# Dense products of a hybrid decoder layer: split and evacuation passes over 1024 columns, pair sums in neighbouring PSUM banks, and six gate-row chunks placed inside the input projection

## The chip, the cores and the metric

The kernel runs on one core of a Trainium2 chip. The metric is the device time of one execution in microseconds. Three executions of the kernel before gave 1505.12, 1505.9 and 1506.55 us, so the median is 1505.9 us; less is better.

## The reference

One decoder layer for 256 tokens of width 2048, all in float32. What matters here, cut from the reference:

```python
mod = c_act @ w_ada[l] + b_ada[l]
sh1, sc1, g1, sh2, sc2, g2 = jnp.split(mod, 6, axis=-1)
h = _modulate(_rmsnorm(x, norm1_g[l]), sh1, sc1)
proj = h @ w_in[l]                       # 256 x 2048 by 2048 x 4928
...
o_a = ...                                # gated linear recurrence, 8 heads, from four blocks of proj
qh = (_rmsnorm(q_a, q_a_norm_g[l]) @ w_q_up[l])
kv = (_rmsnorm(kv_a, kv_a_norm_g[l]) @ w_kv_up[l])
o_b = ...                                # causal attention, 8 heads
mix = jnp.concatenate([o_a, o_b], axis=-1) @ w_out[l]
x = x + g1[:, None, :] * mix
h2 = _modulate(_rmsnorm(x, norm2_g[l]), sh2, sc2)
y = _hier_moe(h2, ...)                   # top 2 of 8 experts in the best of 4 groups
x = x + g2[:, None, :] * y
```

`mod` is a vector of six pieces of 2048: shifts, scales and gates of the two halves of the layer. It is called "ada" below, after its weights.

## The kernel before, in words

**Weights.** All weights come through one ring of buffers of 128 x 4096 float32 (2 MB each). The list `items` gives the order; `ring_fill` (L172) issues the next load on SyncE's queue as soon as a buffer is free, and `ring_done` frees a buffer when the last instruction that reads it has ended. The ring has four buffers (`RING`), two more from the first pieces of the output projection on, and a seventh from the experts on. The experts read 192 chunks in a fixed order, 403 MB of the 571 MB that pass through this queue.

**Dense products.** `dense` (L410 to L435) multiplies 256 tokens by 320 to 512 columns, in the manner of float32 on fp32r matmuls: both factors are split in a high and a low part, and three products are summed. For each 128 rows of weights (`kt`) ScalarE writes the high part (L417), VectorE writes the low part (L418), and TensorE runs six matmuls of 512 columns (L432 to L434, three for each half of the tokens) or, turned, twelve of 256 columns (L425 to L427). The two sums stand in two PSUM tiles of one bank each (`pw`, four buffers), so two products can be in flight. The function `end` empties them: in the input projection ScalarE copies (L455) or VectorE adds to the sum so far (L457), one instruction for each bank.

**Input projection.** `w_in` handles ten blocks of columns in four quarters of the rows, the first quarter in two halves. Beside it, `adt_chunk` works out the shifts and scales of the first norm on VectorE: 24 instructions over 2048 columns (L271), two to a weight chunk, at lower priority than the rest.

**Other ada chunks.** `ada_chunk` (L283 to L296) multiplies the other four pieces (`g1`, `sh2`, `sc2`, `g2`, eight chunks of 2 MB each) on TensorE with one output row, into a bank of their own. A chunk is eight matmul instructions, which the trace records as 16. `EARLY` and `SPREAD` say after which items of the list how many of these 32 chunks stand. `ada_end` empties the bank; for `g1` these are four additions of one row on VectorE (L302).

**Order.** The instructions of each engine are put in order by the scheduler of the tile framework from the program order, priorities and buffers. Each engine then runs its list in order and waits where a semaphore is missing.

**Stages.** Input projection until about 235 us; attention (`mla`) and recurrence (`hgrn`), two of each, with the last quarter of the input projection, until about 450 us; output projection (`w_out`) until about 560 us; routing; then the experts.

Of the kernel before, what the change touches and what calls it, by code (L numbers as in the profile page):

```python
# [17 lines left out]
P = 128  # L18
D = 2048

RING, NARENA, NTEMP, NSPLIT, RING2 = 4, 14, (8, 6), 4, 2

SPREAD = (1, 4, 7, 5, 5, 2, 0, 0, 0, 2, 1, 1, 0)
EARLY = {33: 1}
# [21 lines left out]
def tile_hybrid_layer(ctx, tc, A, out):  # L46
# [6 lines left out]
    psum = ctx.enter_context(tc.tile_pool(name="psum", bufs=1, space=PSUM))  # L53
    late = ExitStack()
# [26 lines left out]
    def pw(name="pw"):  # L81
        return psum.tile([P, 512], F32, tag="w", bufs=4, name=nm(name))
# [327 lines left out]
    def dense(wt, ncol, kts, lhs, end, turned=False):  # L410


        ps = [pw("pacc") for _ in range(2)]
        for i, kt in enumerate(kts):
            w = wt[:, i * ncol:i * ncol + ncol]
            s = splits.tile([P, 2, 512], F32R, tag="s", name=nm("split"))
            S.activation(s[:, 0, :ncol], w, AF.Copy)  # L417
            V.tensor_sub(s[:, 1, :ncol], w, s[:, 0, :ncol])  # L418
# [16 lines left out]
        end(ps)  # L435

    def w_in(it):
# [5 lines left out]
        for n in ns:  # L443
# [6 lines left out]
            def end(ps):  # L450
                if fresh:
                    proj[n] = big([P, 2, 512], "proj")
                for t in range(2):
                    if fresh:
                        S.activation(proj[n][:, t, :ncol], ps[t][:, :ncol], AF.Copy)  # L455
                    else:
                        V.tensor_add(proj[n][:, t, :ncol], proj[n][:, t, :ncol], ps[t][:, :ncol])  # L457
# [109 lines left out]
    def w_out(half, j):  # L567
# [6 lines left out]
        def end(ps):  # L574
            if half == 0:
                mix0[j] = big([P, 2, 512], "mix0")
                for t in range(2):
                    S.activation(mix0[j][:, t], ps[t], AF.Copy)
                return
            m = mix0.pop(j)  # L580
            for t in range(2):
                V.tensor_add(m[:, t], m[:, t], ps[t])
                V.tensor_mul(m[:, t], m[:, t], gate[:, 512 * j:512 * j + 512])
                V.tensor_add(x2[j][:, t], x2[j][:, t], m[:, t])
# [122 lines left out]
    def mla(g):  # L707
# [11 lines left out]
        def keep(dst, n, o):  # L719

            def end(ps):
                for t in range(2):
                    S.activation(dst[:, t], ps[t][:, :n], AF.Copy)
                    if o is None:
                        continue
                    sq = tmp([P, 512], "sq")
                    S.activation(sq[:, :n], ps[t][:, :n], AF.Square)
# [139 lines left out]
    split_stack.close()  # L867
    ringC = late.enter_context(tc.tile_pool(name="ringC", bufs=1, side="right"))
# [338 lines left out]
```

## Time and profile before

| what | value |
|---|---|
| median of three runs | 1505.9 us |
| the profiled execution, its own time | 1505.27 us |
| its span, first to last instruction | 1503.0 us |
| mean granted TensorE clock | 0.888 of full speed |
| TensorE matmul busy | 1127.9 us, 75% |
| VectorE busy | 588.6 us, 39% |
| ScalarE busy | 338.4 us, 23% |
| bytes moved by DMA | 575.61 MB, 383 GB/s over the span |

The profile shows one execution. Busy time is the union of an engine's instructions. A matmul's row lasts longer than the distance to the next matmul's start, since matmuls overlap, so the pace of TensorE is read from starts. The chain is followed back from the last instruction to what released each step. [...]

### The profile page before, as it was taken

The numbers are of one execution on the slowest core, as the hardware profiler recorded it, in microseconds if no ns is written. First come the engines' busy times: TensorE is split into PE (matmuls) and PEld (weight loads), VectorE is DVE, ScalarE is ACT, GpSimd is POOL, SyncE is SP. The second block draws the span as 40 slices with busy tenths as digits, with TensorE's granted clock in tenths as the row PEclk, the third lists the DMA queues.
The fourth block names the chain that finished last, engine by engine and source line by source line (L and its number), as shares of the span: only waits on it lengthen the run. The fifth ranks groups of instructions, "written<-read, shape, count | busy, mean of one in ns | idle before, by whom it ended". The sixth has DMA issues, their size and how long they took to land.

```text
span 1503.0 us, 22846 instructions
## 1 busy us (share of the span) xinstructions
PE 1127.9 (75%) x9893; PEld 687.8 (46%) x9893; DVE 588.6 (39%) x1200; ACT 338.4 (23%) x699; POOL 5.0 (0%) x9
## 2 busy tenths in 40 slices
PE   5989999979999989675666666657657756666556
PEld 2868887737568756333323323323423423332222
DVE  4699998769765552220120121113112112112112
ACT  5634446536435423000100100100100100000000
POOL 0000000000000000000000000000000000000000
PEclk7999999989999999888888888879888889779787
DMA  9788796877979798999999999999999999999995
GB/s 373 263 332 356 298 352 257 315 302 313 369 293 376 293 373 343 430 429 430 430 430 430 430 430 429 429 431 430 430 430 430 430 431 430 430 429 429 431 430 222
DMA packets 44143, 575.61 MB, mean 383 GB/s; under 512 B 4858, under 2 KB 5114, under 8 KB 8712
## 3 DMA queue, kind: packets, MB, share of 16 engines
q1 hardware_dynamic: 42496, 570.56, 91.4%
q10 hardware_dynamic: 1544, 3.56, 0.6%
q8 instruction: 79, 1.29, 0.3%
q14 instruction: 24, 0.20, 0.0%
HBM read 572.00 MB, written 2.11 MB: 382 GB/s over the span
## 4 chain that ended last, share of the span: by engine, by line
DMA 51%; PE 37%; DVE 9%; ACT 1%; issue 1%; SPq 0%; ACTq 0%; DVEq 0%
DMA wch<-in_w_gu_dram 37%; DMA wch<-in_w_down_dram 13%; PE pgu L1040 5%; PE pacc L433 5%; PE pacc L434 5%; PE pacc L432 5%; PE pada L293 3%; PE py L1016 3%; PE pcmb L993 2%; PE pgat L970 2%; DVE wch L271 2%; DVE split L418 2%; DVE proj L457 1%; PE pacc L427 1%; PE pacc L425 1%; PE pacc L426 1%
## 5 line engine op out<-in xcount | busy, mean ns | idle before, releaser
L1040 PE MATMUL pgu<-wch,XT 128*32 128x256 f32 x4096 | 309.7, 455 | 201.0 <-DMA wch<-in_w_gu_dram 201.0
L1040 PEld LDWEIGHTS pgu<-wch,XT 128*32 128x32 f32 x4096 | 139.2, 126 | 361.0 <-DMA wch<-in_w_gu_dram 253.9
L1016 PE MATMUL py<-wch,hT 128*32 128x256 f32 x2048 | 167.9, 485 | 76.8 <-DMA wch<-in_w_down_dram 72.1
L1020 DVE TENSOR_TENSOR Y<-py,gate 32x256 f32<-32x256 f32 x256 | 107.6, 420 | 216.5 <-PE py L1016 213.6
L1005 DVE TENSOR_TENSOR hid<-sgu,pgu 128x128 f32<-128x128 f32 x32 | 9.2, 287 | 462.2 <-ACT sgu L1003 462.2
L418 DVE TENSOR_TENSOR split<-wch,split 128x512 fp32r<-128x512 f32 (+2 forms) x248 | 159.5, 666 | 69.6 <-ACT split L417 69.0
L417 ACT ACTIVATE split<-wch 128x512 fp32r<-128x512 f32 (+2 forms) x248 | 148.0, 614 | 161.2 <-PE pacc L434 98.4
L1016 PEld LDWEIGHTS py<-wch,hT 128*32 128x32 f32 x2048 | 78.9, 133 | 155.0 <-issue 60.8
L1003 ACT ACTIVATE sgu<-pgu 128x128 f32<-128x128 f32 x32 | 8.9, 277 | 602.5 <-PE pgu L1040 602.5
L975 ACT ACTIVATE XT<-pgat,sh,a 128x128 f32<-128x128 f32 x128 | 48.1, 456 | 223.1 <-PE pgat L970 223.0
L433 PE MATMUL pacc<-split,hhi 128*128 128x512 f32 (+1 forms) x192 | 75.5, 393 | 7.0 <-DVE split L418 7.0
L425 PE MATMUL pacc<-hhi,split 128*128 128x256 f32 x256 | 72.4, 286 | 2.8 <-ACT hhi L388 2.2
L426 PE MATMUL pacc<-hlo,split 128*128 128x256 f32 x256 | 72.7, 285 | 1.7 <-DVE hlo L389 1.7
L434 PE MATMUL pacc<-split,hlo 128*128 128x512 f32 (+1 forms) x192 | 73.7, 386 | 0.0
L432 PE MATMUL pacc<-split,hhi 128*128 128x512 f32 (+1 forms) x192 | 72.9, 392 | 0.8 <-DVE proj L457 0.7
L427 PE MATMUL pacc<-hhi,split 128*128 128x256 f32 x256 | 72.2, 285 | 1.1 <-DVE split L418 1.1
L293 PE MATMUL pada<-wch,ca 128*1 128x512 f32 x512 | 68.7, 602 | 3.3 <-DVE pada L288 3.3
L993 PE MATMUL pcmb<-Y,pwt 128*128 128x512 f32 x128 | 59.2, 605 | 15.5 <-DVE Y L1020 15.5
L970 PEld LDWEIGHTS pgat<-ohr,x 128*128 128x128 f32 x512 | 63.4, 205 | 10.7 <-issue 9.8
L970 PE MATMUL pgat<-ohr,x 128*128 128x128 f32 x512 | 66.8, 291 | 0.7 <-DVE sm L937 0.7
L271 DVE SCALAR_TENSOR_TENSOR wch<-wch,gate 128x2048 f32<-128x2048 f32 x24 | 54.8, 2284 | 0.0
L457 DVE TENSOR_TENSOR proj<-proj,pacc 128x512 f32<-128x512 f32 (+1 forms) x80 | 51.2, 662 | 0.8 <-PE pacc L434 0.4
(311 smaller groups left out, 1215.4 us busy)
## 6 DMA issues: line engine op xcount, KB each, us to landing
wch<-in_w_gu_dram SPq DMA_DIRECT2D x128, 2048.0 KB, 31.1
wch<-in_w_down_dram SPq DMA_DIRECT2D x64, 2048.0 KB, 31.5
wch<-in_w_ada_dram SPq DMA_DIRECT2D x36, 2048.0 KB, 10.1
wch<-in_w_ada_t_dram SPq DMA_DIRECT2D x12, 2048.0 KB, 7.9
wch<-in_w_in_dram SPq DMA_DIRECT2D x12, 2048.0 KB, 9.2
wch<-in_w_out_dram SPq DMA_DIRECT2D x8, 2048.0 KB, 9.5
wch<-in_w_in_h_dram SPq DMA_DIRECT2D x8, 1024.0 KB, 8.9
wch<-in_w_in_dram SPq DMA_DIRECT2D x3, 1664.0 KB, 7.0
```

The source lines that it names most:

```text
L293: PE.matmul(acc[b][32 * j:32 * j + 1, :], ca[:, kt:kt + 1], w[:, o:o + 512], start=kt == 0, stop=kt == 15)
L417: S.activation(s[:, 0, :ncol], w, AF.Copy)
L418: V.tensor_sub(s[:, 1, :ncol], w, s[:, 0, :ncol])
L426: PE.matmul(o, s[:, 0, c], lo, start=False, stop=False, skip_group_check=True)
L432: PE.matmul(o, hi[:, c], s[:, 0, :ncol], start=first, stop=False)
L433: PE.matmul(o, hi[:, c], s[:, 1, :ncol], start=False, stop=False)
L434: PE.matmul(o, lo[:, c], s[:, 0, :ncol], start=False, stop=stop)
L970: PE.matmul(ps[:, 128 * i:128 * i + 128], x2[kt // 4][:, t, 128 * (kt % 4):128 * (kt % 4) + 128], ohr[:, t], start=t == 0, stop=t == 1)
L993: PE.matmul(ps, PWT[G4][:, 128 * t:128 * t + 128], Y4[j // 2][:, 512 * (j % 2):512 * (j % 2) + 512], start=True, stop=True)
L1016: PE.matmul(py[32 * j:32 * j + 32, :256], H["T"][:, 32 * kt:32 * kt + 32], w[:, 1024 * kt + 256 * j:1024 * kt + 256 * j + 256], start=kt = ...
L1020: V.tensor_mul(Y[q][r:r + 32, 256 * j:256 * j + 256], py[32 * j:32 * j + 32, :256], gate[32 * j:32 * j + 32, c:c + 256])
L1040: PE.matmul(gu[32 * j:32 * j + 32, :256], XT[G4][kt // 8][:, kt % 8, 32 * e4:32 * e4 + 32], w[:, 1024 * i + 256 * j:1024 * i + 256 * j + 2 ...
```

## The change

Each split pass now covers 1024 columns where the weights allow it: two `kt` of 512 columns, four of 256, or two of 320 (640 columns). The split buffers are three of 1024 columns, where there were four of 512. The two sums of a product are one PSUM tile of two neighbouring banks, in a pool of two such tiles that is closed before the experts; an evacuation is one instruction over both banks. In the second half of the output projection three of four blocks are finished with instructions over 1024 columns, and the last one as before. The small temporary tiles are five, before six. The lists move five more of the `g1` chunks into the input projection: six stand there (after items 10, 17, 20, 24, 29 and 33 of the list), before one; after the items that follow there are 0, 3, 6, 5, 3, 2 in place of 1, 4, 7, 5, 5, 2.

```diff
-RING, NARENA, NTEMP, NSPLIT, RING2 = 4, 14, (8, 6), 4, 2
+RING, NARENA, NTEMP, NSPLIT, RING2 = 4, 14, (8, 5), 3, 2
-SPREAD = (1, 4, 7, 5, 5, 2, 0, 0, 0, 2, 1, 1, 0)
-EARLY = {33: 1}
+SPREAD = (0, 3, 6, 5, 3, 2, 0, 0, 0, 2, 1, 1, 0)
+EARLY = {10: 1, 17: 1, 20: 1, 24: 1, 29: 1, 33: 1}
...
-        ps = [pw("pacc") for _ in range(2)]
+        acc2 = psum_dense.tile([P, 2, 512], F32, tag="d", name=nm("pacc"))
+        ps = [acc2[:, 0], acc2[:, 1]]
+        some = 1024 // ncol // 2 * 2
         for i, kt in enumerate(kts):
-            w = wt[:, i * ncol:i * ncol + ncol]
-            s = splits.tile([P, 2, 512], F32R, tag="s", name=nm("split"))
-            S.activation(s[:, 0, :ncol], w, AF.Copy)
-            V.tensor_sub(s[:, 1, :ncol], w, s[:, 0, :ncol])
+            if i % some == 0:
+                n = ncol * min(some, len(kts) - i)
+                both = splits.tile([P, 2, 1024], F32R, tag="s", name=nm("split"))
+                w = wt[:, i * ncol:i * ncol + n]
+                S.activation(both[:, 0, :n], w, AF.Copy)
+                V.tensor_sub(both[:, 1, :n], w, both[:, 0, :n])
+            s = both[:, :, i % some * ncol:(i % some + 1) * ncol]
...
-        end(ps)
+        end(acc2)
...
-                for t in range(2):
-                    if fresh:
-                        S.activation(proj[n][:, t, :ncol], ps[t][:, :ncol], AF.Copy)
-                    else:
-                        V.tensor_add(proj[n][:, t, :ncol], proj[n][:, t, :ncol], ps[t][:, :ncol])
+                dst, src = proj[n][:, :, :ncol], ps[:, :, :ncol]
+                if fresh:
+                    S.activation(dst, src, AF.Copy)
+                else:
+                    V.tensor_add(dst, dst, src)
```

**VectorE, input projection, where the first `adt` passes run.** Before (`split` is the low part, L418; `proj` the sum so far, L457; `adt` a pass over 2048 columns, L271):

```order
L457 TENSOR_TENSOR proj_251<-proj_251,pacc_584 128x512
L418 TENSOR_TENSOR split_652<-wch_522,split_652 128x512
L457 TENSOR_TENSOR proj_251<-proj_251,pacc_585 128x512
L418 TENSOR_TENSOR split_661<-wch_522,split_661 128x512
L271 SCALAR_TENSOR_TENSOR wch_443,adt_642<-wch_443,gate 128x2048
L457 TENSOR_TENSOR proj_274<-proj_274,pacc_618 128x512
L457 TENSOR_TENSOR proj_274<-proj_274,pacc_619 128x512
```

and now (L424, L464 and L273 are the same three lines):

```order
L464 TENSOR_TENSOR proj_268<-proj_268,pacc_566 128x1024
L424 TENSOR_TENSOR split_606<-wch_523,split_606 128x1024
L424 TENSOR_TENSOR split_623<-wch_523,split_623 128x1024
L464 TENSOR_TENSOR proj_300<-proj_300,pacc_605 128x1024
L273 SCALAR_TENSOR_TENSOR wch_583,adt_653<-wch_583,gate 128x2048
```

Each pair of passes of 512 columns is one of 1024; the `adt` passes stand between them as they did.

**TensorE, the same place of the input projection.** The first of the six early chunks (`pada`) now stands between two products (before, no `pada` stood in this part of the list):

```order
L439 MATMUL pacc_566<-split_567,hhi_210 128x512
L440 MATMUL pacc_566<-split_567,hhi_210 128x512
L441 MATMUL pacc_566<-split_567,hlo_211 128x512
L295 MATMUL pada_593<-wch_485,ca 1x512 x8
L439 MATMUL pacc_605<-split_606,hhi_210 128x512
```

**VectorE, end of `g1`.** Before, its four additions (`brows`, L302) stood among the passes of the first recurrence (`b`, `d`: L501 to L504) and the end of the first attention (`o`, `mlo`):

```order
L201 TENSOR_SCALAR sm_2547<-sm_2547 128x8
L302 TENSOR_TENSOR brows_99<-brows_99,pada_1936 1x512
L202 TENSOR_TENSOR sm_2545<-sm_2545,sm_2547 128x8
L503 TENSOR_TENSOR d_478_2834<-b_2833 128x1024
L818 TENSOR_TENSOR o_2445<-o_2445,sm_2545 128x1024
L302 TENSOR_TENSOR brows_99<-brows_99,pada_1936 1x512 x3
```

and now they stand earlier, in the softmax of the first attention (`s`, `pT`):

```order
L806 TENSOR_REDUCE sm_2196<-s_2194 128x4
L464 TENSOR_TENSOR proj_268<-proj_268,pacc_2363 128x1024
L807 TENSOR_SCALAR sm_2196<-sm_2196 128x4
L304 TENSOR_TENSOR brows_102<-brows_102,pada_593 1x512 x4
L424 TENSOR_TENSOR split_2437<-wch_2395,split_2437 128x1024
L816 COPY pT_2208<-ppT_2203 128x512
```

They moved from behind the scan of the recurrence to ahead of the copy of the probabilities.

## Rows read from the trace of the kernel before

**Rows 1.** The page: span, and each engine's busy time.
```profile
span 1503.0 us, 22846 instructions
PE 1127.9 (75%) x9893; PEld 687.8 (46%) x9893; DVE 588.6 (39%) x1200; ACT 338.4 (23%) x699; POOL 5.0 (0%) x9
```

**Rows 2.** Stretches: length, busy time of PE, PEld, DVE, ACT, POOL, granted clock, DMA share, GB/s.
```profile
66.00:145.00 79.00, 70.15 (x414) 59.09 (x412) 77.26 (x125) 32.81 (x57) 0.00 (x0) 0.98 0.87 336
145.00:235.00 90.00, 87.22 (x526) 74.65 (x530) 83.37 (x141) 43.36 (x76) 0.00 (x0) 1.00 0.82 317
292.00:314.00 22.00, 14.30 (x109) 10.50 (x108) 20.00 (x35) 10.27 (x17) 0.95 (x1) 0.83 0.84 329
314.00:397.00 83.00, 81.83 (x538) 52.42 (x539) 55.59 (x112) 42.40 (x85) 0.96 (x1) 0.98 0.81 325
397.00:416.00 19.00, 13.13 (x109) 7.72 (x108) 18.91 (x33) 9.40 (x13) 0.42 (x1) 1.00 0.87 334
460.00:560.00 100.00, 98.65 (x509) 68.61 (x507) 54.61 (x99) 42.37 (x82) 0.00 (x0) 1.00 0.86 341
...
600.00:1503.00 903.00, 580.60 (x6413) 288.05 (x6413) 166.59 (x373) 56.00 (x165) 0.00 (x0) 0.84 0.99 421
```

**Rows 3.** The chain that ended last, from 160 to 225 us, shares by line.
```profile
by line: PE pacc L433 18.9%; PE pacc L434 18.5%; PE pacc L432 16.7%; PE pacc L426 11.6%; PE pacc L427 11.5%; PE pacc L425 11.2%; issue 3.6%; DVE proj L457 2.8%; DVE split L418 2.0%; ACT split L417 2.0%; DVE hlo L389 0.9%; DVE wch L271 0.2%;
```

**Rows 4.** The chain from 225 to 320 us, then from 320 to 460 us.
```profile
by line: PE pada L293 13.9%; PE pacc L434 11.8%; PE pacc L432 11.5%; PE pacc L433 11.2%; PE psc L788 2.8%; PE psc L786 2.8%; DVE brows L302 2.8%; DVE proj L457 2.6%; DVE b L501 2.5%; PE pov L810 2.2%; PE pqa L667 2.1%; PE pqk L765 2.0%; ACT
...
by line: PE pada L293 16.6%; PE pacc L432 11.9%; PE pacc L433 11.3%; PE pacc L434 10.8%; PE po L549 4.8%; PE po L551 4.2%; PE pA L527 3.5%; PE pov L810 2.2%; PE psc L786 1.9%; PE psc L788 1.9%; DVE split L418 1.9%; DVE b L501 1.7%; PE pqk L
```

**Rows 5.** Groups of VectorE from 66 to 145 us: count, busy, mean ns, idle before.
```profile
L271 DVE SCALAR_TENSOR_TENSOR wch<-wch,gate 128x2048 f32<-128x2048 f32 x14 | 32.0, 2284 | 0.0
L418 DVE TENSOR_TENSOR split<-wch,split 128x512 fp32r<-128x512 f32 x41 | 26.4, 684 | 0.3 <-ACT split L417 0.2
L457 DVE TENSOR_TENSOR proj<-proj,pacc 128x512 f32<-128x512 f32 x30 | 19.8, 682 | 0.2 <-PE pacc L434 0.2
```

**Rows 6.** Timeline of VectorE: start, length; runs of 512 columns, then passes of 1024.
```profile
66.89 1.89 DVE L418 TENSOR_TENSOR split<-wch,split 128x512 fp32r<-128x512 f32 x3
...
73.38 1.28 DVE L457 TENSOR_TENSOR proj<-proj,pacc 128x512 f32<-128x512 f32 x2
...
306.56 1.21 DVE L503 TENSOR_TENSOR d<-b 128x1024 f32<-128x1024 f32 x1
307.70 1.21 DVE L818 TENSOR_TENSOR o<-o,sm 128x1024 f32<-128x1024 f32 x1
308.94 2.09 DVE L302 TENSOR_TENSOR brows<-brows,pada 1x512 f32<-1x512 f32 x3
```

**Rows 7.** Timeline of TensorE in dense products: start, length.
```profile
481.98 0.40 PE L432 MATMUL pacc<-split,mhi 128*128 128x512 f32 x1
482.21 0.40 PE L433 MATMUL pacc<-split,mhi 128*128 128x512 f32 x1
```

**Rows 8.** The chain in order of time: one ada chunk on TensorE, start and length.
```profile
275.48 1.83 PE pada L293 x16
```

**Rows 9.** Groups from 60 to 225 us: matmuls that wait for the low part.
```profile
L433 PE MATMUL pacc<-split,hhi 128*128 128x512 f32 x104 | 42.7, 411 | 7.0 <-DVE split L418 7.0
```

**Rows 10.** ScalarE from 0 to 600 us: passes over 512 and over 1024 columns.
```profile
L417 ACT ACTIVATE split<-wch 128x512 fp32r<-128x512 f32 x224 | 137.7, 631 | 148.3 <-PE pacc L434 86.4 <-PE pacc L427 30.2 <-DMA wch<-in_w_in_dram 11.6
L506 ACT ACTIVATE d<-d 128x1024 f32<-128x1024 f32 x2 | 2.1, 1060 | 0.1
```

More of the change, by code (lines that the diff above doesn't have):

```diff
@@ L53, in tile_hybrid_layer @@
     psum = ctx.enter_context(tc.tile_pool(name="psum", bufs=1, space=PSUM))
+    dense_stack = ExitStack()
+    psum_dense = dense_stack.enter_context(tc.tile_pool(name="psum_dense", bufs=2, space=PSUM))
     late = ExitStack()
@@ L81, in pw @@
     def pw(name="pw"):
-        return psum.tile([P, 512], F32, tag="w", bufs=4, name=nm(name))
+        return psum_late.tile([P, 512], F32, tag="w", name=nm(name))
     def bc(ap, shape):
@@ L576, in end @@
                 mix0[j] = big([P, 2, 512], "mix0")
-                for t in range(2):
-                    S.activation(mix0[j][:, t], ps[t], AF.Copy)
+                S.activation(mix0[j], ps, AF.Copy)
                 return
             m = mix0.pop(j)
[L581 to L584, printed above, removed]
+            g = gate[:, 512 * j:512 * j + 512]
+            if j < 3:
+                V.tensor_add(m, m, ps)
+                V.tensor_mul(m, m, bc(g[:, None, :], [P, 2, 512]))
+                V.tensor_add(x2[j], x2[j], m)
+            else:
+                for t in range(2):
+                    V.tensor_add(m[:, t], m[:, t], ps[:, t])
+                    V.tensor_mul(m[:, t], m[:, t], g)
+                    V.tensor_add(x2[j][:, t], x2[j][:, t], m[:, t])
             x2_ready(j)
@@ L721, in end @@
             def end(ps):
+                S.activation(dst, ps[:, :, :n], AF.Copy)
+                if o is None:
+                    return
                 for t in range(2):
-                    S.activation(dst[:, t], ps[t][:, :n], AF.Copy)
-                    if o is None:
-                        continue
                     sq = tmp([P, 512], "sq")
-                    S.activation(sq[:, :n], ps[t][:, :n], AF.Square)
+                    S.activation(sq[:, :n], ps[:, t, :n], AF.Square)
                     V.tensor_reduce(ss[:, o + 4 * t:o + 4 * t + 4], sq[:, :n].rearrange("p (a b) -> p a b", a=4), AX.X, OP.add)
@@ L867, in tile_hybrid_layer @@
     split_stack.close()
+    dense_stack.close()
+    psum_late = late.enter_context(tc.tile_pool(name="psum_late", bufs=4, space=PSUM))
     ringC = late.enter_context(tc.tile_pool(name="ringC", bufs=1, side="right"))
```

## The prediction

> **What bounds the kernel now.** I read the page first [rows 1]: no engine is busy for more than 75% of the span, so the bound changes on the way. The stretches come next [rows 2]. From 600 us on the DMA engines are busy for 0.99 of the time at 421 GB/s: the experts stream weights and nothing else counts there. Their volume is fixed, so the whole kernel ends earlier by just as much as the part before 600 us ends earlier, and only that part can gain. Its bound alternates. From 66 to 145 us (stretch A) VectorE is busy 77.26 of 79 us and TensorE 70.15: VectorE is the bound. From 145 to 235 us (B) the chain is TensorE's own dense matmuls, 88% of it between 160 and 225 us [rows 3], though VectorE is at 83.37 of 90. From 225 to 460 us (C) the chain is mostly TensorE again, and its largest line is the ada matmuls, 13.9% and 16.6% [rows 4], with two islands (292 to 314 and 397 to 416 us) where VectorE is at 20.00 of 22 and 18.91 of 19 and TensorE idles. From 460 to 560 us (D) TensorE is at 98.65 of 100. DMA stays at 317 to 341 GB/s in these stretches, against 421 behind them.
>
> **Merged passes.** Their gain is smaller than mean durations suggest. Two passes of 684 ns against one of 1.21 us would be 0.16 us, but passes overlap: three splits run in 1.89 us, of which the last is 0.69, so one follows the other after 0.60; two additions out of PSUM take 1.28, the same step of 0.60 [rows 6]. A pass of 1024 is followed by the next after 307.70 − 306.56 = 1.14 us. A pair costs 1.20 before and 1.13 to 1.14 after: 0.07 us saved. A pass from PSUM over two banks has no row; at worst it saves nothing (two steps of 0.60), at best about this 0.07, which I take, since at 512 columns PSUM and SBUF cost the same.
> In A there are 41 splits and 30 additions of 512 columns [rows 5], some 35 pairs: 35 × 0.07 = **2.5 us off**, on the path because VectorE is the bound. The islands of C hold about six pairs: **0.4 us off**. In B, D and the rest of C TensorE leads and VectorE's saving is hidden behind it: 0. If that cover went, nothing would be added, since the passes only get shorter.
> [...]
> ScalarE's pass grows from 631 to about 1060 ns [rows 10] and halves in number. It is busy 32.81 of 79 us in A, so this costs nothing as long as a split is ready before TensorE asks. TensorE's six matmuls start 0.233 us apart [rows 7], so one `kt` lasts 1.40 us and a merged pair covers 2.80 us, against 1.06 on ScalarE and 1.14 on VectorE. With three buffers, two pairs (5.6 us) can be ready ahead, before three `kt` (4.2 us); an `adt` pass that stands between splits holds VectorE for 2.28 us. That can only shorten the 7.0 us of matmuls that waited for a low part [rows 9]; I book nothing for it and keep up to 7 us as the bound on the good side.
>
> **Moved ada chunks.** Five chunks leave C. One is 16 matmul records in 1.83 us [rows 8], so 9.15 us of TensorE. The chain holds ada matmuls for 13.9% of 95 us and 16.6% of 140 us, 13.2 + 23.2 = 36.4 us, of the 24 chunks × 1.83 = 43.9 us that stand there: 83% of an ada chunk is on the path. 9.15 × 0.83 = **7.6 us off**. Bounds: 9.15, and about 2 if the scheduler had put just these chunks into gaps.
> They come back in the input projection. By the dense matmuls that stand ahead of them in the changed list, three of the five fall into A and two into B. In A TensorE has 79 − 70.15 = 8.85 us free, and three chunks take 5.5: hidden, and 5.5 at most if that cover is gone. In B TensorE leads: 2 × 1.83 = **3.7 us added**, 0 at the least if they fill its gaps.
> Their loads move too: 5 × 2.1 MB, three of them (6.3 MB) into A. A moved 79 × 336 GB/s = 26.5 MB; now 32.8 MB in 76.5 us is 429 GB/s, just above the 421 of the experts' stage. At 60 us the ring is full, up to 8 MB ahead, and that credit brings the need to about 325 GB/s if it is all spent; so I take 0, and the case where it doesn't hold is a rival. In C the loads get thinner.
> SyncE's queue only issues loads, in the order of the list; five loads of C that stood ahead of other weights no longer do, which can help only.
>
> **The end of g1.** Three of its four additions took 2.09 us and the fourth 0.6 in the first island, where VectorE is the bound [rows 2, 6]. They leave it: 2.6 off at most. They now stand ahead of the copy of the probabilities in the first attention, where TensorE has other work; taking half, **1.3 us off**, with 0 as the other end.
>
> **Fewer temporaries, both banks in one tile.** Five small tiles in place of six can make a pass wait for a buffer; no row shows it, and I take 0, with a bound of 3 us (some five passes of 0.60).
>
> **Sum.** −2.5 − 0.4 − 7.6 + 3.7 − 1.3 = −8.1 us. The profiled execution took 1505.27 us (its span and 2.3 us around it), which leaves 1497.2; the median of the runs lies 0.6 above it, so the forecast is **1497.5 us**.
>
> **Rivals.**
> *DMA becomes the bound of A (slower).* A needs 429 GB/s without the ring's credit. No stretch of the front came near that: D, the best, had 341 GB/s [rows 2]. If A moves only 380 GB/s, midway between that and 421, its 32.8 MB take 86.3 us, 9.8 more than the 76.5 of the sum: −8.1 + 9.8 = +1.7, and 1507.6 us on the median; at 360 GB/s 91.1 us and 1512.4. It decides as soon as the ring runs empty at the `adt` chunks. For: four buffers and items of unequal use. Against: the full ring at the start. 0.13.
> *The late evacuation (slower).* Before, the first bank could be emptied while the last three matmuls (0.70 us) wrote the second. Now the pass waits for both. If VectorE, in order, stands waiting for each of A's 15 products, that is 10.5 us: 1508.3. Against: its list has splits and `adt` passes of 2.28 us in between, and [rows 5] show 0.2 us of waiting for sums. [...] 0.04.
> *Twice the gain.* The two chunks in B fill gaps (−3.7) and the longer lead of the splits takes 5 of the 7.0 us of waits: −8.1 − 8.7, 1489. For: VectorE at 83.37 of 90 in B means that some of its waits matter. 0.20.
> *No change.* The chunks in C were filling gaps of the attention's chain, so only 2 us come off, and the additions of `g1` only change place: −2.5 − 0.4 − 2 + 3.7 = −1.2, 1504.7. For: the chain follows what ran last, and an idle TensorE would have waited just as long for VectorE. 0.13.
>
> **How the numbers follow.** The forecast has 0.50. 0.2% is 3 us, about what a measurement of this kernel can tell from no change. Faster by more: 0.46 of the forecast's 0.50, all 0.20 of the double gain, 0.04 of the no-change case: 0.70. Slower by more than 0.2%: of the two slow rivals 0.11, whose milder forms stay inside it, and 0.02 of the forecast, by its bad bounds: 0.13. The rest, 0.17, is the same. The range takes in the forecast with its bounds, the double gain and the no-change case, and the nearer part of the slow rivals: 1485 to 1508.
>
> **What would show it.** Split and addition passes near 1.21 us with a step of 1.14; VectorE still the bound of A and A about 2.5 us shorter; ada on the chain of C at some 29 us in place of 36.4; the end of `g1` out of the first island; A near 425 GB/s. I would be wrong in the mechanism if A's chain shows loads, if matmuls wait longer for splits than before, or if C is no shorter though its chunks are gone.

## The result, and the profile after

The changed kernel takes 1527.59 us (median of four runs, 1521.61 to 1528.19); the kernel before, on the same chip, 1506.22 us. The ratio is 1.0132 with a 95% interval of 1.0106 to 1.0159: **slower by 21 us**, where 8 us less were forecast.

The profiled execution took 1521.61 us by its own time, the other three 1527.52 to 1528.19, so some 5 of the 21 us are in no trace. The page of the changed kernel, span and busy times as in [rows 1]:

```profile
span 1519.3 us, 22410 instructions
PE 1127.9 (74%) x9893; PEld 689.9 (45%) x9893; DVE 574.8 (38%) x1025; ACT 313.6 (21%) x551; POOL 5.0 (0%) x9
```

VectorE has 13.8 us less work in 175 instructions fewer, and TensorE exactly as much, yet the span grew by 16.3 us. Two marks split it: the first matmul of the attention (`pqa`) ends the input projection, and the first one of the router (`pgat`) stands ahead of the experts. Before, they start at 238.6 and 566.0 us; now at 270.4 and 582.0. The input projection grew by 31.8 us, the stages between the marks shrank by 15.8, and what follows is as long as it was (937.0 and 937.3 us). Stretches of the changed kernel, in the columns of [rows 2]:

```profile
66.00:145.00 79.00, 65.75 (x394) 52.80 (x394) 64.63 (x77) 23.61 (x29) 0.00 (x0) 0.94 0.90 361
145.00:235.00 90.00, 80.94 (x478) 68.17 (x478) 71.83 (x79) 31.49 (x36) 0.00 (x0) 0.96 0.84 333
```

In A (66 to 145 us) VectorE is busy 64.63 of 79 us, where it was 77.26; TensorE 65.75, where it was 70.15. No engine bounds the stage any more, and the DMA engines, at 361 GB/s, don't either (e9 below moves 401). Groups of VectorE in A, as in [rows 5]:

```profile
L273 DVE SCALAR_TENSOR_TENSOR wch<-wch,gate 128x2048 f32<-128x2048 f32 x12 | 27.4, 2283 | 1.2 <-DMA wch<-in_w_ada_t_dram 1.2
L424 DVE TENSOR_TENSOR split<-wch,split 128x1024 fp32r<-128x1024 f32 x18 | 21.4, 1219 | 2.2 <-ACT split L423 2.2
L464 DVE TENSOR_TENSOR proj<-proj,pacc 128x1024 f32<-128x1024 f32 x13 | 15.8, 1219 | 11.1 <-PE pacc L441 7.8 <-PE pacc L434 3.1
```

A pass over 1024 columns lasts 1219 ns, as forecast. What is new is the last column: 11.1 us in which VectorE stood ahead of a sum that TensorE had not finished, where [rows 5] have 0.2. The chain of A says the same; first before, then the changed kernel:

```profile
by line: DVE wch L271 31.9%; DVE split L418 23.2%; DVE proj L457 19.3%; issue 7.3%; PE pacc L433 5.3%; PE pacc L434 4.4%; PE pacc L432 1.9%; DVE hlo L389 1.6%; ACT split L417 1.6%; PE pacc L427 0.9%; DVE sh L277 0.9%; DVE a L281 0.6%; DVE a
```

```profile
by line: DVE wch L273 14.0%; PE pacc L440 12.4%; PE pacc L441 11.6%; PE pacc L439 10.9%; DVE split L424 8.9%; PE pacc L434 8.5%; PE pacc L432 7.6%; PE pacc L433 7.5%; issue 5.6%; DVE proj L464 4.7%; ACT split L423 2.7%; PE pada L295 2.3%; P
```

Before, it was one engine's line of work; now it changes between VectorE and TensorE, each waiting for the other. The waits from 60 to 240 us (engine and line, what for, us in total, times, longest) of the kernel before:

```profile
DVE split L418 <- ACT split L417: 7.7, 16, 0.9
ACT h L385 <- DVE sh L277: 7.4, 3, 6.1
ACT h L385 <- DVE a L281: 5.6, 4, 3.9
```

and of the changed kernel:

```profile
ACT h L387 <- DVE a L283: 52.3, 7, 11.3
DVE split L424 <- ACT split L423: 11.7, 13, 1.7
DVE proj L464 <- PE pacc L434: 10.9, 5, 3.6
DVE proj L464 <- PE pacc L441: 10.4, 10, 2.2
ACT split L423 <- DMA wch<-in_w_in_dram: 6.9, 2, 4.4
```

The longest of them, 11.27 us, in the timeline (ScalarE, then VectorE, then TensorE):

```profile
143.25 0.56 ACT L387 ACTIVATE h<-pxT,sh,a 128x256 f32<-128x256 f32 x1 [11.27 <-DVE a L283]
143.71 1.05 ACT L423 ACTIVATE split<-wch 128x1024 fp32r<-128x1024 f32 x1
...
139.32 1.22 DVE L464 TENSOR_TENSOR proj<-proj,pacc 128x1024 f32<-128x1024 f32 x1 [2.17 <-PE pacc L434]
140.46 0.15 DVE L279 TENSOR_TENSOR sh<-adt,pc 128x1 f32<-128x1 f32 x1
140.53 2.29 DVE L273 SCALAR_TENSOR_TENSOR wch<-wch,gate 128x2048 f32<-128x2048 f32 x1
143.05 0.16 DVE L283 SCALAR_TENSOR_TENSOR a<-a,pc 128x1 f32<-128x1 f32 x1
144.79 1.23 DVE L424 TENSOR_TENSOR split<-wch,split 128x1024 fp32r<-128x1024 f32 x1 [1.58 <-ACT split L423]
...
139.21 1.90 PE L295 MATMUL pada<-wch,ca 128*1 128x512 f32 x16
143.86 0.65 PE L384 MATMUL pxT<-cst,x 128*128 128x128 f32 x4 [2.75 <-ACT h L387]
```

ScalarE's list has `h` next, which needs `a`; the `adt` pass that gives `a` stands in VectorE's list behind a sum that waits for TensorE; and behind `h` stands the split that TensorE needs next. TensorE finishes its early chunk at 141.1 and idles 2.75 us. Each engine keeps to its list, and the lists don't fit each other.

### The profile page after: what moved, and what is told of

It reads as the page before. It is cut to its first block, busy times and chain, and to the rows that moved or that the text cites. A ratio compares the mean times of both kernels' runs of the same rounds, so it can differ in the third digit from the quotient of the medians.

```text
span 1519.3 us, 22410 instructions
## 1 busy us (share of the span) xinstructions
PE 1127.9 (74%) x9893; PEld 689.9 (45%) x9893; DVE 574.8 (38%) x1025; ACT 313.6 (21%) x551; POOL 5.0 (0%) x9
## 4 chain that ended last, share of the span: by engine, by line
DMA 50%; PE 38%; DVE 8%; ACT 3%; issue 1%; SPq 0%; ACTq 0%; DVEq 0%
DMA wch<-in_w_gu_dram 37%; DMA wch<-in_w_down_dram 10%; PE pgu L1054 5%; PE pacc L440 5%; PE pacc L441 5%; PE pacc L439 5%; PE pcmb L1007 4%; PE py L1030 3%; PE pada L295 2%; PE pacc L434 2%; DVE split L424 2%; PE pacc L433 1%; DVE wch L273 1%; PE pacc L432 1%; ACT split L423 1%; DMA wch<-in_w_ada_dram 1%
## 5 line engine op out<-in xcount | busy, mean ns | idle before, releaser
L424 DVE TENSOR_TENSOR split<-wch,split 128x1024 fp32r<-128x1024 f32 (+1 forms) x122 | 144.3, 1195 | 78.9 <-ACT split L423 78.7
L423 ACT ACTIVATE split<-wch 128x1024 fp32r<-128x1024 f32 (+1 forms) x122 | 125.0, 1035 | 138.2 <-PE pacc L441 94.7
L440 PE MATMUL pacc<-split,hhi 128*128 128x512 f32 (+1 forms) x192 | 77.1, 402 | 7.9 <-DVE split L424 7.9
L439 PE MATMUL pacc<-split,hhi 128*128 128x512 f32 (+1 forms) x192 | 76.2, 397 | 5.0 <-ACT split L423 3.2
L432 PE MATMUL pacc<-hhi,split 128*128 128x256 f32 x256 | 74.6, 291 | 6.2 <-ACT hhi L390 2.2
L434 PE MATMUL pacc<-hhi,split 128*128 128x256 f32 x256 | 74.5, 291 | 5.1 <-DVE split L424 5.1
L295 PE MATMUL pada<-wch,ca 128*1 128x512 f32 x512 | 65.5, 592 | 0.4 <-DMA wch<-in_w_ada_dram 0.4
L464 DVE TENSOR_TENSOR proj<-proj,pacc 128x1024 f32<-128x1024 f32 (+1 forms) x40 | 47.1, 1177 | 23.9 <-PE pacc L441 12.8
L273 DVE SCALAR_TENSOR_TENSOR wch<-wch,gate 128x2048 f32<-128x2048 f32 x24 | 54.7, 2284 | 1.2 <-DMA wch<-in_w_ada_t_dram 1.2
## 6 DMA issues: line engine op xcount, KB each, us to landing
wch<-in_w_out_dram SPq DMA_DIRECT2D x8, 2048.0 KB, 10.2
```

The lines of the kernel that those rows point to most:

```text
L295: PE.matmul(acc[b][32 * j:32 * j + 1, :], ca[:, kt:kt + 1], w[:, o:o + 512], start=kt == 0, stop=kt == 15)
L423: S.activation(both[:, 0, :n], w, AF.Copy)
L424: V.tensor_sub(both[:, 1, :n], w, both[:, 0, :n])
L434: PE.matmul(o, s[:, 1, c], hi, start=False, stop=stop, skip_group_check=True)
L439: PE.matmul(o, hi[:, c], s[:, 0, :ncol], start=first, stop=False)
L440: PE.matmul(o, hi[:, c], s[:, 1, :ncol], start=False, stop=False)
```

## The experiments

All runs, each against the kernel before on its own chip. "Projection" is the start of the first `pqa` matmul, "middle" the time from there to the first `pgat` matmul, both read from the one profiled execution of a run. One such reading is uncertain by about 0.7 us: e19 already runs that much behind the kernel before at 60 us, ahead of its first moved chunk.

| run | median us | ratio [95%] | projection | middle |
|---|---|---|---|---|
| before | 1506.2 | 1 | 238.6 | 327.4 |
| changed | 1527.59 | 1.0132 [1.0106, 1.0159] | 270.4 | 311.6 |
| e1 lists only | 1517.04 | 1.0077 [1.0060, 1.0094] | 262.4 | 314.8 |
| e2 merges only | 1515.06 | 1.0060 [1.0043, 1.0077] | 245.2 | 329.9 |
| e3 two-bank sums only | 1512.69 | 1.0043 [1.0026, 1.0060] | 242.6 | 331.4 |
| e4 merged splits only | 1508.25 | 1.0010 [0.9999, 1.0020] | 239.5 | 327.4 |
| e5 lists, spare buffers | 1529.9 | 1.0155 [1.0138, 1.0172] | 274.1 | 315.7 |
| e6 changed, `h` later | 1525.03 | 1.0122 [1.0094, 1.0150] | 276.9 | 311.0 |
| e8 two-bank tile, fine passes | 1512.33 | 1.0041 [1.0026, 1.0055] | 243.4 | 329.9 |
| e9 old order, 10.5 MB more | 1508.37 | 1.0017 [1.0007, 1.0026] | 240.4 | 328.7 |
| e10 lists, old order | 1509.17 | 1.0020 [1.0011, 1.0030] | 252.6 | 316.2 |
| e11 lists, their order, thin loads | 1516.55 | 1.0066 [1.0049, 1.0083] | 263.9 | 315.4 |
| e12 changed, old order | 1517.09 | 1.0062 [1.0046, 1.0079] | 266.1 | 312.4 |
| e13 merges, old order | 1521.3 | 1.0098 [1.0081, 1.0115] | 253.4 | 328.5 |
| e14 e5 in the old order | 1513.72 | 1.0048 [1.0031, 1.0065] | 258.9 | 316.0 |
| e15 e8 in the old order | 1523.7 | 1.0112 [1.0095, 1.0129] | 255.1 | 330.3 |
| e16 changed, `adt` early | 1526.41 | 1.0136 [1.0119, 1.0153] | 274.6 | 311.5 |
| e17 before, `adt` early | 1511.18 | 1.0031 [1.0020, 1.0041] | 245.0 | 326.7 |
| e18 e10 with thin loads | 1505.39 | 0.9992 [0.9983, 1.0002] | 249.5 | 315.8 |
| e19 two chunks, old order | 1514.24 | 1.0051 [1.0036, 1.0066] | 246.8 | 329.1 |

**The parts of the change.** Each alone in the kernel before: the lists (e1), all merges (e2), two-bank tiles with one evacuation pass (e3), merged splits (e4).

```diff
+SPREAD = (0, 3, 6, 5, 3, 2, 0, 0, 0, 2, 1, 1, 0)
+EARLY = {10: 1, 17: 1, 20: 1, 24: 1, 29: 1, 33: 1}
...
+        acc2 = psum_dense.tile([P, 2, 512], F32, tag="d", name=nm("pacc"))
+                V.tensor_add(dst, dst, src)
...
+            if i % some == 0:
+                both = splits.tile([P, 2, 1024], F32R, tag="s", name=nm("split"))
```

> The kernel before with the new lists alone: five more g1 chunks in the input projection, passes of 512 columns and the sums in single banks as before. Theory H (the merged passes changed the order on ScalarE, so that the activation that makes h, which waits for a scale from VectorE, stands ahead of splits that TensorE needs): this kernel keeps the fine passes, so it is no slower; ScalarE waits for the scale at the h activation for under 25 us in the input projection (13 us before, 60 us after the change), and with the chunks out of the attention it takes 1494 to 1503 us. Rival D (the ada chunks in the input projection crowd the loads or TensorE there): 1515 us or more, the input projection ends 15 us or more later than before, and the matmuls or passes there wait for loads.

> The changed kernel with the old lists: all merged passes, but only one early g1 chunk. Theory H: the input projection ends about as late as in the changed kernel (25 to 35 us after before), ScalarE waits 40 us or more at the h activations, and without the gain in the attention the kernel takes 1525 to 1545 us. Rival D: the input projection is as short as before, 1500 to 1508 us.

> Only the evacuation is merged (both banks in one tile, one pass out of them); splits of 512 columns in four buffers, six small temporaries, old lists. Theory H: ScalarE's splits stay fine, so an h activation in the wrong place holds back less, 1503 to 1513 us. Rival E (the evacuation of both banks at once starts too late, and VectorE, in order, stands before it): VectorE waits 15 us or more at the additions and the kernel takes 1515 us or more.

> Only the splits are merged (three buffers of 1024 columns, five small temporaries); each bank is emptied by itself, old lists. Theory H: here the order on ScalarE is coarse, ScalarE waits 30 us or more at the h activations and the kernel takes 1515 to 1540 us. Rival E: VectorE's additions are as before, so 1500 to 1508 us.

Theory H failed. From 60 to 240 us `h` waits 41.8 us for `a` in e1, with fine passes, where under 25 were expected; 20.8 in e2 and 16.9 in e4, with merged ones, where 40 and 30 or more were. Only e3 came out inside H's range. Rival D's times came true in e1, but not its reason: ScalarE waits 9.1 us for loads there, 10.2 before. In e2 its times failed too. Rival E of e3 expected 15 us of waits at the additions; they are 3.9.

The lists cost 10.8 us, the merges 8.8; together 19.6 of the 21.4 of the whole. In the lists, the projection pays 23.8 us and the middle gives back 12.6. Of the merges, the merged splits change nothing that the runs can tell (e4), and the two-bank tile 4 us in the projection and as much behind it. With fine passes out of the same tile:

```diff
-                V.tensor_add(dst, dst, src)
+                for t in range(2):
+                    V.tensor_add(dst[:, t], dst[:, t], src[:, t])
```

> As the run with the merged evacuation alone (1512.7 us), with the two sums in one tile of two banks, but emptied by two passes of 512 columns, as before the change. Theory T (the tile of two banks costs the time: the passes out of it and the next product wait for both banks): 1510 to 1515 us. Rival P (the single pass costs it: it starts when the second bank is done and holds VectorE for 1.14 us): 1503 to 1508 us.

The same 1.004: the loss comes with the tile, not with the wider pass. The tile also brought another order, to which e15 below comes back.

**Two theories that fell.** The place of `h` in ScalarE's list, moved back by a priority (e6), and the slots of the ring, saved by loading the five early chunks in quarters into idle temporaries (e5):

```diff
+            with tc.high_priority(-120):
                 S.activation(h32[:, i], ps[:, 256 * i:256 * i + 256], AF.Identity, scale=a1[:, kt:kt + 1],
...
+        spare[it] = [tmp([P, 1024], "spare") for _ in range(4)]
+            nc.sync.dma_start(t, A["w_ada"][0, it[2], :, 1024 * m:1024 * m + 1024])
```

> The changed kernel with the passes that make h (two activations, high and low part) at a lower priority for the scheduler, so that on ScalarE they stand behind some more splits; passes, buffers and lists are those of the changed kernel (1527.6 us, ScalarE waits 60 us at h). Theory H (the place of h in ScalarE's list costs the time): the wait at h falls below 35 us and it takes 1508 to 1518 us. Rival R (the scale comes late because its weights come late; the place of h only shows it): the time stays at 1522 to 1532 us.

> The new lists on the fine passes (as the run with the lists alone, 1517 us, where the input projection ended 23.8 us late and the part behind it was 12.6 us shorter), but the five moved g1 chunks do not pass through the ring of four buffers: each is loaded as four pieces of 0.5 MB into four large temporaries that lie idle in the input projection. Bytes, matmuls and queue are the same. Theory R (an extra item in the ring takes a buffer from the weights that VectorE and TensorE wait for; 23.8 / 5 = 4.8 us a chunk): the projection's transposes of q start at 238 to 248 us, and the kernel takes 1494 to 1502 us. Rival B (the bytes or TensorE's time are the price, 2.1 MB at 430 GB/s being 4.9 us): they start at 258 us or later and it takes 1512 to 1520 us.

Neither gained: 276.9 and 274.1 us. But neither is a clean test. In e6 `h` still waits 49.8 us for `a`, where under 35 were expected, so its place was hardly moved. In e5 the loads in quarters cut the early chunks' matmuls into small groups: the ada matmuls of its projection take 21.4 us of TensorE, 11.4 in e1. And nothing that was done to the work had left the lists of instructions alone, which the next runs do.

**Bytes or order.** In the next runs each engine's list in the input projection is held to what it is in the kernel before, by a dependency without a semaphore between neighbours of the old list:

```diff
+    for e, order in ORDER.items():
+        for i, j in zip(order, order[1:]):
+            tc.add_manual_dep(chain[e][j], chain[e][i].name, mybir.DependencyInfo(
+                mybir.DependencyClass.NoSync, mybir.DependencyReason.DATA), reason="order")
```

To this e9 adds five loads that nothing reads, e10 the new lists; e11 has the lists and the order of e1, and loads an eighth of the early chunks:

```diff
+            nc.sync.dma_start(t, A["w_ada"][0, it, :, 1024 * m:1024 * m + 1024])
...
+            if items[i] in thin:
+                src, cols = src[:, :512], 512
```

> The kernel before, with the order of every instruction on TensorE, VectorE and ScalarE held to what it is there, and five more loads of 2.1 MB on SyncE's queue in the input projection, at the places of the list where the changed kernel loads its five more gate chunks, into temporaries that are idle there. Nothing reads them; the output is complete. Two theories of why the input projection is 23.8 us longer with the new lists alone. (1) Bytes: a load more costs what it takes to move, 2.1 MB at 430 GB/s = 4.9 us, as the transfers are what the stage follows: the input projection ends 15 to 24 us later than before (238.6 us), at 254 to 263, and the run takes 1521 to 1530 us, since nothing leaves the stages behind. (2) Order: the scheduler, which models the loads, put the passes and the matmuls in another order, and the waits between the engines come from that: with the old order the input projection ends at 239 to 244 us; the five loads are then 10.5 MB more in stages that had room, and the run takes 1506 to 1512 us.

> The new lists alone (passes and banks as before), as in the run with the lists alone, but in the input projection the instructions that both kernels have are held to the order of the kernel before, on TensorE, VectorE and ScalarE; only the early chunks' matmuls stand between. (1) Bytes: the input projection ends at 258 to 265 us, as with the lists alone (262.4), and the run takes 1514 to 1520 us. (2) Order: it ends at 240 to 250 us (before 238.6, and 5 x 1.83 = 9.2 us of matmuls where TensorE leads), and the run takes 1495 to 1506 us, since the attention keeps its gain of about 12 us.

> The new lists alone, with exactly the order of that run on TensorE, VectorE and ScalarE, but the five early chunks load an eighth of their bytes (512 of 4096 columns, 9.2 MB less in all) and their matmuls read those columns eight times; the gate rows of these chunks are left out of what is computed. Slots of the ring, matmuls and places are the same. (1) Bytes: the input projection ends 14 to 22 us earlier than with the lists alone (262.4), at 240 to 248 us. (2) Order: it ends at 257 to 263 us, and only the loads behind gain.

The projection of e9 ends at 240.4 us, as theory (2) has it: 10.5 MB more cost 1.8 us when the order stays. Its stretches:

```profile
60.00:120.00 60.00, 52.08 (x302) 43.51 (x302) 56.91 (x91) 25.78 (x48) 0.00 (x0) 0.97 0.99 401
120.00:180.00 60.00, 55.97 (x342) 48.98 (x341) 56.39 (x93) 27.89 (x47) 0.95 (x1) 1.00 1.01 411
```

The DMA engines are full, at 401 and 411 GB/s, where before they moved 336 and 318, and VectorE is as busy as it was. In e11 the bytes are gone and the time isn't: 263.9 us. Its waits from 60 to 240 us:

```profile
ACT h L421 <- DVE a L317: 43.0, 9, 9.0
DVE proj L493 <- PE pacc L463: 7.2, 7, 1.5
DVE proj L493 <- PE pacc L470: 2.7, 2, 1.5
```

beside those of the lists alone (e1):

```profile
ACT h L385 <- DVE a L281: 41.8, 9, 8.4
DVE proj L457 <- PE pacc L427: 7.2, 7, 1.5
DVE proj L457 <- PE pacc L434: 2.7, 2, 1.5
```

They are the same waits, as often and nearly as long. And with the chunks and all their bytes but the old order (e10) they are not there:

```profile
ACT split L451 <- DMA wch<-in_w_in_dram: 14.1, 3, 5.4
ACT h L419 <- DVE sh L311: 6.3, 2, 5.6
ACT h L419 <- DVE a L315: 5.4, 5, 2.1
DVE wch L305 <- DMA wch<-in_w_ada_t_dram: 5.1, 3, 2.3
DVE proj L491 <- PE pacc L461: 0.2, 1, 0.2
```

So 9.8 of the 23.8 us (262.4 − 252.6) are order. The other 14.0 come with the chunks, and put e10 behind the 240 to 250 us that were expected; e18 holds the old order and thins the loads, to tell matmuls from loads:

> The new lists with the order of the kernel before held in the input projection, as in the run with lists and old order (its end 252.6 us, 1509.17), but the five early chunks load an eighth of their bytes and read those columns eight times; their gate rows are left out of what is computed. If the last 3 us are waits for loads (14.1 + 5.1 us of waits for transfers on ScalarE and VectorE in that run), the input projection ends at 247 to 250 us: the matmuls' 9.2 us alone. If they come from where the matmuls stand, it ends at 251 to 254 us.

At 249.5 us, 10.9 us stay without the bytes. That is inside the 247 to 250 us of the first theory, but not by the 9.2 us that it names, as the ada matmuls from 60 to 245 us show, in the kernel before, e10 and e18:

```profile
L293 PE MATMUL pada<-wch,ca 128*1 128x512 f32 x32 | 3.8, 591 | 0.0
L327 PE MATMUL pada<-wch,ca 128*1 128x512 f32 x96 | 12.4, 591 | 0.0
L330 PE MATMUL pada<-wch,ca 128*1 128x512 f32 x96 | 14.8, 591 | 0.0
```

Before, not one but two chunks (32 records, at 212 and 234 us) stand ahead of the first `pqa`, since one of the chunks that `SPREAD` places runs early enough too; now there are six. And the scheduler placed them anew: one group of 16 records takes 1.83 us to the next start, but a group of two to eight takes 0.95 to 0.97, and e18 has eleven groups, e10 seven, e1 six. So the matmuls add 8.6 us in e10 and 11.0 in e18, about all of its 10.9. If they are paid in full, 5.4 of e10's 14.0 us are left, and they go with the bytes; how is open, since ScalarE waits 21.5 us for loads in e18 too, against 14.1.

The lists of e10 and of the kernel before are the same but for the chunks, so one matmul can be followed through both. At 60 us e10 is 0.1 us ahead. Near the end of A, before and in e10:

```profile
144.15 0.63 PE L432 MATMUL pacc<-split,hhi 128*128 128x512 f32 x2
151.57 0.63 PE L466 MATMUL pacc<-split,hhi 128*128 128x512 f32 x2
```

It starts 7.4 us later behind three chunks, whose matmuls take 5.5: nothing of them is hidden in A. Where e18 ties with the kernel before, it leaves out 9.2 MB.

**The old order elsewhere.** The changed kernel (e12) and the merges alone (e13) with VectorE's and ScalarE's old order (TensorE's left to the scheduler), the spare buffers of e5 (e14, all three engines held), and the two-bank tile of e8 (e15, held as e12):

> The changed kernel whole, but in the input projection the passes of VectorE and ScalarE are held to the order of the kernel before (a merged split at the place of the first of its parts, a merged sum at the place of the last); TensorE's order and the place of the early chunks stay with the scheduler. (1) The order is what costs: the input projection ends at 250 to 258 us (changed kernel 270.4, before 238.6; the lists alone with the old order 252.6), the waits of h for a fall from 59.7 to about 15 us, and the run takes 1505 to 1514 us. (2) Merged passes and two-bank sums cost by themselves (a coarse pass or a sum that waits for both banks): the input projection ends at 262 to 270 us and the run takes 1518 to 1527 us.

> Merged passes and two-bank sums with the old lists, as in the run with the merges alone (1515.06, input projection to 245.2), but in the input projection the passes of VectorE and ScalarE are held to the order of the kernel before, as in the run beside it. (1) Order: the input projection ends at 237 to 241 us (before 238.6); what the merges cost behind it (2.5 us) stays, and the run takes 1506 to 1510 us. (2) The merges cost by themselves: it ends at 243 to 247 us and the run takes 1512 to 1516 us.

> The new lists, the five early chunks loaded into temporaries that are idle there (as in the run with spare buffers, 1529.9), so that they take no slot of the ring, and the input projection held to the order of the kernel before on TensorE, VectorE and ScalarE. With the ring's slots and this order its end was 252.6 us. If the slots cost the 3 us that neither the matmuls (9.2) nor the bytes (1.8) explain, it ends at 248 to 251 us and the run takes 1503 to 1507 us; if not, at 252 to 255 us and 1507 to 1511 us. If the order had not been what made the first run with spare buffers so slow (274.1), it ends at 268 to 275 us.

> The kernel before with both sums of a product in one tile of two banks, but still one evacuation pass for each bank (as in the run with the two-bank tile, 1512.33, input projection to 243.4), and the passes of VectorE and ScalarE in the input projection held to the order of the kernel before; TensorE's order is the scheduler's, since the old one starts a product in a bank whose neighbour is not yet emptied. (1) The tile costs by what it makes wait (the next product for both banks): the input projection ends at 242 to 250 us and the run takes 1509 to 1517 us. (2) It costs by the order of the passes that came with it: 238 to 240.5 us and 1506 to 1509 us.

e14 is 15.2 us earlier than e5, with the same loads, buffers and work, though not at the 248 to 251 that would make the ring's slots the last 3 us (VectorE there waits 9.4 us for sums, 0.5 in e10). But that doesn't clear the slots. Five of its chunks are cut into groups, nearly all of four records:

```profile
L336 PE MATMUL pada<-spare,ca 128*1 128x512 f32 x80 | 19.3, 591 | 0.0
```

With the sixth chunk that is 21.2 us, 8.8 more than in e10, and the projection is only 6.3 longer; what the slots are worth stays open.

In e12 the wait of `h` for `a` fell as theory (1) has it, from 59.7 to 19.0 us, but the projection gained only 4.3 where I expected 12 or more. ScalarE's splits now wait 37.4 us for loads, 6.9 in the changed kernel:

```profile
L445 ACT ACTIVATE split<-wch 128x1024 fp32r<-128x1024 f32 (+1 forms) x52 | 52.0, 1018 | 88.2 <-DMA wch<-in_w_in_dram 37.4 <-PE pacc L463 20.7 <-PE pacc L456 19.7
```

By the medians e12 is 10.5 us faster than the changed kernel, whose profiled execution was its fastest, and lies between the two theories. e13 and e15 went the other way, by 8.2 and 11.7 us: the expectation failed. With the tile and the old lists, the old order of passes is a bad one. Waits of e15 from 60 to 240 us:

```profile
DVE proj L487 <- PE pacc L463: 8.6, 11, 1.4
DVE proj L487 <- PE pacc L456: 3.7, 7, 1.4
```

The old order empties one bank, does other work, and empties the second (the order rows of VectorE ahead of the prediction show it); the next product could start in the first. A tile of two banks takes that away, which fits the waits for sums (0.4 us in the kernel before) but isn't tested by itself. Whether its 4 to 5 us in e3 and e8 are this wait or only the other order that came with it, these runs don't tell.

**Order by itself.** The `adt` passes at normal priority, in the changed kernel (e16) and in the kernel before (e17):

```diff
-            with tc.high_priority(-120):
+            with tc.high_priority(0):
```

> The changed kernel with the adt passes at the same priority as the rest, in place of a lower one; this moves them forward in VectorE's list by a few instructions and leaves TensorE's list nearly as it is (48 of some 2500 rows differ). Order theory: h waits less for a (59.7 us in the changed kernel, now below 45), the input projection ends at 258 to 267 us (270.4), and the run takes 1512 to 1524 us. If the order of the passes is not what costs, it ends at 269 us or later and the run takes 1526 us or more.

> The same move in the kernel before: nothing but the priority of the adt passes, so the same work, bytes, passes and banks in another order. If the order that the scheduler happens to give is worth microseconds, the input projection ends outside 236 to 241 us, more likely later (242 to 252), and the run takes 1508 to 1520 us; if order is worth little, it ends at 237 to 241 us and the run takes 1504 to 1509 us.

e17 is the plainest run of all: the same instructions, bytes and buffers, and 6.4 us more in the projection, inside the 242 to 252 us of the order theory. The one edit changed the lists of all three engines. Its waits:

```profile
ACT h L385 <- DVE a L281: 19.1, 8, 4.2
DVE split L418 <- ACT split L417: 9.8, 20, 1.3
DVE proj L457 <- PE pacc L434: 3.8, 4, 1.5
```

e16 is no repair: `h` waits 58.7 us for `a`, as long as without the move (59.7, both up to the end of the projection), and the projection ends 4.2 us later in the profiled executions, while the medians are alike (1526.41 and 1527.59); that expectation failed too. Last, a try for a faster version, two more early chunks in place of five:

```diff
-SPREAD = (1, 4, 7, 5, 5, 2, 0, 0, 0, 2, 1, 1, 0)
-EARLY = {33: 1}
+SPREAD = (0, 3, 7, 5, 5, 2, 0, 0, 0, 2, 1, 1, 0)
+EARLY = {24: 1, 29: 1, 33: 1}
```

> Only two more early chunks, after items 24 and 29 (three early ones with the old one after 33), the rest of the lists as before but for two chunks fewer in the attention, passes and banks as before, and the input projection held to the order of the kernel before. By the measured prices a chunk costs 2.8 us in the input projection (14.0 for five) and gives back 2.2 to 2.5 in the attention: the input projection ends at 243 to 245 us and the run takes 1505 to 1509 us, no change. If the two late places are better ones, where the ring is not short of loads, a chunk costs its 1.83 us: end at 241 to 243 us, run 1503 to 1506 us.

It missed on both sides: 8.2 us more in the projection, and the middle no shorter. The middle could give little. Only one chunk crosses the mark, since three stand ahead of it and two did before, and the ada matmuls behind it take 64.8 us of TensorE, 64.9 before; in e1, with four chunks fewer, 54.7. No version beats the kernel before.

## Why the prediction was wrong

**Merged passes, 2.5 us off.** The size was right: in the changed kernel a sum out of two banks starts at 82.56 and the next instruction at 83.69, a step of 1.13 against 1.20 for a pair.

```profile
82.56 1.22 DVE L464 TENSOR_TENSOR proj<-proj,pacc 128x1024 f32<-128x1024 f32 x1
83.69 0.15 DVE L279 TENSOR_TENSOR sh<-adt,pc 128x1 f32<-128x1 f32 x1
```

A split pass out of SBUF has the same step, from 87.18 to 88.31. So both sources save the 0.07 us that the rows gave. What failed is "on the path because VectorE is the bound": with merged splits alone the projection ends no earlier (0.8 us later in e4, about what a single trace can tell). VectorE was the bound of A by a list in which it never had to wait, and that list went with the edit.

**The longer lead of the splits**, up to 7.0 us on the good side, gave nothing: from 60 to 260 us of the changed kernel the matmuls of L440 and L434 wait 7.9 and 5.1 us for a low part, where [rows 9] had 7.0.

**Chunks that leave the middle, 7.6 us off, with 0.4 and 1.3 more.** Right in kind, and too small: 12.6 us off with the lists alone, 11 to 13 in every run with the five chunks moved and the passes fine. I had held 9.15 us, the matmuls' own time, to be the most, at the 1.83 us of an uncut chunk. But most chunks there are cut: from 225 to 460 us the 24 of the kernel before keep TensorE busy for 51.8 us and not the 43.9 of the sum, and from 270 to 475 us the 19 of the changed kernel for 41.4, which is 10.4 off. The chain of the changed kernel's middle, from 270 to 350 and from 350 to 475 us:

```profile
by line: DMA wch<-in_w_ada_dram 9.8%; DMA wch<-in_w_in_dram 9.7%; PE pada L295 9.6%; PE pacc L440 9.0%; PE pacc L439 8.9%; PE pacc L441 8.7%; ACT split L423 4.9%; PE pov L822 4.6%; PE ppT L814 3.3%; PE psc L798 2.9%; PE psc L800 2.7%; PE pa
...
by line: PE pada L295 11.7%; PE pacc L439 8.5%; PE pacc L440 7.9%; PE pacc L441 7.8%; PE po L556 5.2%; PE po L558 4.7%; DVE split L424 3.8%; ACT split L423 3.2%; PE pA L534 2.5%; PE psc L800 2.1%; PE psc L798 2.1%; DVE kn L518 2.0%; DVE b L
```

Ada matmuls hold 9.6% of 80 and 11.7% of 125 us of it, 7.7 + 14.6 = 22.3 us; I expected 29. Two loads stand on the chain in their place, 9.8% and 9.7% of 80, so not all that the chunks left was gained.

**Chunks that come into the projection, 3.7 us.** The step "in A TensorE has 8.85 us free, and three chunks take 5.5: hidden" failed: by the end of A e10 is 7.4 us late behind three chunks, and e18, almost without bytes, pays 10.9 us where its ada matmuls take 11.0 more. TensorE's free time in A was waiting for VectorE, in between matmuls that others wait for; a chunk put there delays the next sum, and with it VectorE. That is argued from the lists; that the time is paid is measured. The case "if that cover is gone" was priced at 5.5 and left out of the sum.

**The ring's credit, "I take 0".** Measured at 1.8 us for the bytes alone (e9) and about 5.4 in the ring with the chunks (what e10 pays beyond its matmuls, an estimate). A did not run at 425 GB/s but at 361. *DMA becomes the bound of A* would have given the right sign, by a mechanism that is not there: from 60 to 180 us e9 took 401 to 411 GB/s, for 1.8 us.

**The late evacuation**, the rival at 0.04, named a row that came true: 10.5 us of VectorE waiting for products in A were worked out, 11.1 are in the trace. It is not the whole cause: with the tile alone the projection is 4.8 us longer (e8), and in e1, with single banks, the sums already wait 7.2 + 2.7 us from 60 to 240 us.

**The missing term: a new order.** Nothing in the sum, and none of the rivals, stood for it. I compared the lists at three places, found the `adt` passes "between them as they did", and priced only what was added and removed. But the scheduler deals all lists anew, and in the projection three engines take turns so closely that the order is worth as much as the work. Five pairs of runs have the same work in another order: e1 and e10 (9.8 us apart), e5 and e14 (15.2), e8 and e15 (11.7), e2 and e13 (8.2), before and e17 (6.4). With the passes and banks of the kernel before, every other order was worse than its own (e1, e5, e17); with the two-bank tile its order of passes was the worse one under the old lists (e13, e15) and the better one under the new (e12).

The account of the projection's 31.8 us: 23.8 by the lists (9.8 order; of the other 14.0 about 8.6 the matmuls as e10 has them, and 5.4 what goes with the bytes), 6.6 by the merges (e2, where work and order aren't told apart), 1.4 by both together. These are single traces, and the last term is near their noise. A small slip beside it: 1497.2 + 0.6 is 1497.8, where the forecast says 1497.5. That the lists' new order comes from the loads as the scheduler models them is argued, not shown. And whether the merges in a good order would cost nothing stays open: the two orders tried for them were worse than the scheduler's.

## What to carry to other kernels

Where a scheduler orders the instructions of engines that wait for each other every few microseconds, an edit is two changes: the work, and a new order of everything near it; hold the old order by dependencies without semaphores, and the two can be measured apart, as long as the old order still suits the work (in e13 and e15 it did not). An engine's idle time is room for more work only if nobody waits for what stands behind it in its list: of A's 8.85 us, three chunks of 5.5 us in all left e10 7.4 us late. And an engine that is busy for 98% of a stage is the bound under one order, and perhaps under that alone: VectorE was busy for 64.63 of A's 79 us under the new one. Last, a matmul group that is moved can be cut on the way, and then it has another price, as the 1.83 us of a whole group and the 0.95 to 0.97 us of each piece show: read it in every run.

## What the runs showed of the hardware

The DMA engines took 401 to 411 GB/s for 120 us beside TensorE at 0.9 and VectorE at 0.94 of the time, against 336 and 318 before, for 1.8 us on the stage: the share of 0.81 to 0.88 there was room. And a VectorE pass over two neighbouring banks has the same step, 1.13 us, as one over 1024 columns of SBUF. The one-row ada matmuls cost by the group: two to eight records that stand together take 0.95 to 0.97 us to the next start, and ten to sixteen take 1.81 to 1.83 (e5, e10, e14, e18), so that five chunks kept TensorE busy for 19.3 us in e14 and would take 9.2 uncut.
